# RWKV recurrence: the products of b, k with a, r over the 64 rows of their own head

## The chip, the core and the metric

The kernel runs on one core of a Trainium2 chip. The metric is the device time of one execution in microseconds (us). The core's engines run side by side and wait for each other by semaphores: TensorE (PE in the profile; PEld are its weight loads), VectorE (DVE), ScalarE (ACT), GpSimd (POOL), and SyncE (SP), which issues the DMA transfers.

## The reference, cut to what matters

A two-layer decoder trunk over 1024 tokens with 1024 features, batch 1, all in float32. Layer 0 mixes tokens with RWKV-7, layer 1 with sparse attention; each is followed by a SwiGLU. The change touches RWKV-7 alone: 16 heads of 64 features, each with a 64 x 64 state.

```python
def _rwkv7_step(S, inp):
    r_t, w_t, k_t, v_t, a_t, b_t = inp
    sa = jnp.einsum('bhij,bhj->bhi', S, a_t)
    S = S * w_t[:, :, None, :] + sa[..., None] * b_t[:, :, None, :] + v_t[..., None] * k_t[:, :, None, :]
    y = jnp.einsum('bhij,bhj->bhi', S, r_t)
    return S, y
...
    S0 = jnp.zeros((B, H, N, N), f32)
    _, y = lax.scan(_rwkv7_step, S0,
                    (tm(rh), tm(decay), tm(kh), tm(vh), tm(-kk), tm(kk * ah)))
```

## The kernel before

The tokens go in two halves of 512. Each half is first projected, with weights split into two float32r parts (L204, L121 split them; L233 to L235 are the three products), and what the recurrence needs (a, r, b, k, v, all scaled with the decay) is spilled to DRAM. Then the recurrence runs over 16 chunks of 64 tokens. It replaces the scan's steps within a chunk by products of 64 x 64 blocks and an inverse of a unit triangular block, which is computed beforehand (L630, L632, and L655 for the parts between its 32 x 32 blocks).

For a chunk, `load_chunk` brings `cbk` (b and k; feature rows of two heads in the two halves of the 128 partitions, eight pairs p of heads), `car` (a and r, 128 rows each, where for head e of a pair the other head's 64 rows are zeros, written once), `cv` (v) and `ttp` (the inverse). Then:

- `pre_chunk` makes what doesn't depend on the state. For each of the 8 pairs and both heads e, L958 multiplies `cbk[:, p]` (stationary, 128 rows x 128 columns: b's and k's 64 tokens) with `car[:, :, p, e]` (moving, a's and r's 64 tokens each). The contraction is over all 128 rows, 64 of which are the zeros. Two pairs fill one PSUM bank of tag "g". From it DVE takes the masked parts: L962 the products with a, for the 64 rows that this head uses, into `lz` (whose other 64 rows are a itself, copied by POOL at L952), and L964 those with r, into `g1`. L970 transposes `cbk` into `bk`, L978 subtracts the mean from v and puts it into `uv`.
- `chain_chunk` carries the state. L993 (z from `lz` and `uv`), a copy into zs (L995), L999 (with `ttp`), copies into `uv` (L1000, L1001), L1007 (new state from `bk` and `uv`), and L1011, L1012 (state S times its decay), copied into the next chunk's `uv` (L1015, L1016). The output is L1020 (r with the old state) plus L1023 (`g1` with `uv`), in a bank of tag "g".
- `norm` normalises the output of the chunk before: a square (L115), its sum (L1033), L1035, and yn (L1037), which reads the output's bank for the last time; L1040 transposes yn.
- After every four chunks `tail` starts: scale, bonus, gate (L1070 to L1081) and the output projection for those 256 tokens, with the residual R (L801 loads it from x, L802 scales it on DVE). It runs in steps beside the following chunks, as do the merges of the second half's inverses (L655) in the chunks 1 to 4.

PSUM has two banks each for the tags t, u, g and o in this stage. The order of the instructions on each engine is set at build time: a scheduler with a simulated timeline moves instructions where their data and a free buffer allow it. So an edit at one place can change the order at others.

Of the kernel before, what the change touches and what calls it, by code (L numbers as in the profile page):

```python
# [9 lines left out]
F32 = mybir.dt.float32  # L10
# [5 lines left out]
OP = mybir.AluOpType  # L16
# [65 lines left out]
def trunk(ctx, tc, a, out):  # L82
# [13 lines left out]
    def banks(st, name, **bufs):  # L96
        """PSUM banks of a phase by tag"""
        cur.append((pool(st, name, space=PSUM), bufs))
        st.callback(cur.pop)
# [19 lines left out]
    def sub(eng, lo, x, hi):  # L119
        """what the float32r rounding hi of x leaves"""  # L120
        i = eng.tensor_tensor(lo, x, hi.bitcast(F32), op=OP.subtract)  # L121
        (lastv if eng is V else lastg)[0] = i
# [88 lines left out]
    def wcols(w, off, ld, ncol=P):  # L211
        """weights [D, ld] as stationary tiles: columns off..off+ncol of all KT row tiles"""
        st = wst()
        dma(st[:, :KT * ncol].rearrange("p (k n) -> p k n", n=ncol), dap(w, off, [[ld, P], [P * ld, KT], [1, ncol]]))
        kp = 512 // ncol
        hi, lo = split(st, KT * ncol, kp * ncol)
        v = lambda t: [t[k // kp][:, k % kp * ncol:k % kp * ncol + ncol] for k in range(KT)]
        return v(hi), v(lo)

    def wrows(w, k0, nk, col, ld, perm=False):  # L220
        """weights as moving tiles: nk row tiles from k0, 512 columns"""
        st = wst()
        st3 = st[:, :nk * 512].rearrange("p (k n) -> p k n", n=512)
        if perm:
            for b in range(2):
                dma(st3[64 * b:64 * b + 64], dap(w, (k0 + b) * P * ld + col, [[ld, 64], [64 * ld, 2], [1, 512]]))
        else:
            dma(st3, dap(w, k0 * P * ld + col, [[ld, P], [P * ld, nk], [1, 512]]))
        hi, lo = split(st, nk * 512)
        return hi, lo  # L230
# [8 lines left out]
    def proj_fm(w, off, ld, xhi, xlo, ncol=P, c=slice(0, 512)):  # L239
        """[ncol features, tokens c]"""  # L240
        wh, wl = wcols(w, off, ld, ncol)
        o = psx(bank[0])
        for k in range(KT):
            mm3(o[:ncol, c], wh[k], wl[k], xhi[k][:, c], xlo[k][:, c], k == 0, k == KT - 1)
        return o

# [37 lines left out]
    def weave(ga, na, gb, nb):  # L284
        """two generators side by side, in proportion to their lengths"""
        ia = ib = 0
        while ga or gb:
            if ga and (not gb or ia * nb <= ib * na):
                ia += 1
                ga = None if next(ga, ga) is ga else ga  # L290
            else:
                ib += 1
                gb = None if next(gb, gb) is gb else gb

    def ada_v(l, j, stage, tmp):
        """the same with the products summed over the row tiles on VectorE"""
        acc = tmp()
        for k2 in range(4):
            st = stage()
            dma(st.rearrange("p (k n) -> p k n", n=512),  # L300
                dap(a["ada_w"], l * D * 6 * D + 2 * k2 * P * 6 * D + j * 512, [[6 * D, P], [P * 6 * D, 2], [1, 512]]))
            for i in range(2):
                k = 2 * k2 + i
                if k == 0:
                    V.tensor_scalar(acc, st[:, 0:512], csr[:, 0, 0:1], None, op0=OP.mult)
                else:
                    V.scalar_tensor_tensor(acc, st[:, i * 512:i * 512 + 512], csr[:, k, 0:1], acc, op0=OP.mult, op1=OP.add)
        mp = pst()
        for i in range(4):
            mm(mp[:, i:i + 1], acc[:, i * P:(i + 1) * P], ones, start=i == 0, stop=True, skip_group_check=True)  # L310
        V.tensor_tensor(modf[:, l, j * 4:j * 4 + 4], mp[:, 0:4], adb[l][:, j * 4:j * 4 + 4], op=OP.add)
# [11 lines left out]
    def hin_vec(l, s):  # L323
        """per feature scale and shift that take the previous LN's z (or x) to the sub-layer's input"""
# [8 lines left out]
    # position bias by head, distance descending, one row per query of a block, shifted by one place a row  # L333
# [23 lines left out]
    # the gate's second factor with its columns in the order of the normed heads  # L357
# [27 lines left out]
    def rwkv_head(hf, p1, pr, res, xq=None):  # L385
        """hin^T with the previous token in column 0, and what the low-rank branches take from it"""
# [64 lines left out]
    def rwkv_proj(hf, p1, head, between, betweenv):  # L451
# [20 lines left out]
        def low_rank_in():  # L472
            """the small operands twice: their rounding and what it leaves, over the rows of the weights' two parts"""
# [46 lines left out]
        # k  # L520
# [65 lines left out]
        # v  # L586
# [10 lines left out]
        # r  # L597
# [19 lines left out]
    def tinv_dve(hf, tp):  # L617
        """inverses of the unit triangular 64 x 64 blocks: their two 32 x 32 blocks, a unit (chunk, head) per partition"""
# [22 lines left out]
    def tinv_merge(hf, g, tp):  # L641
        """T12 = T1^T (N21^T T2^T) of 32 units, a quarter of the array for 8 of them"""
# [33 lines left out]
    with ExitStack() as st:  # L676
# [8 lines left out]
        def first_chunk():  # L685
            """the first chunk's operands, ahead of the recurrence"""
# [46 lines left out]
        # the first modulation, shift and scale of the first half of the features before those of the second  # L733
# [60 lines left out]
    def resid(l, s, hf, tt, lnt, r=None):  # L794
        """alpha * x of the sub-layer, token major"""
# [43 lines left out]
    def out_pair(w, l, s, hf, q, xh, xl, c, lnt, rr, tp, bk, perm=False, order=NK):  # L839
        """token-major product of two token tiles (columns c of x) with w [D, D], then residual and layer norm, in steps"""  # L840
# [54 lines left out]
    def hin_pair(i, q, zt, hi, lo):  # L895
        """the same for two token tiles that are still on the chip"""
# [17 lines left out]
    if True:  # L914
# [4 lines left out]
        for i in range(2):  # L919
# [3 lines left out]
            if i == 0:  # L923
                lz = [pc.tile([P, KT, 2, 64], F32, name="lz0")]
                first_g1 = [pc.tile([P, 2, P], F32, tag="g10", bufs=4, name="g1") for _ in range(4)]
# [11 lines left out]
        mask_r = cst[:, None, C_M + P:C_M + 2 * P].to_broadcast([P, 2, P])  # L937
# [10 lines left out]
        def pre_chunk(hf, c):  # L948
            """what does not depend on the state"""
# [4 lines left out]
            for p in range(0, KT, 2):  # L954
                o = psg().rearrange("p (i x e t) -> p i x e t", i=2, x=2, e=2)
                for i in range(2):
                    for e in range(2):
                        mm(o[:, i, :, e, :], cbk[:, p + i].rearrange("p a t -> p (a t)"), car[:, :, p + i, e, :], start=True, stop=True)  # L958
                g = first_g1.pop() if first_g1 else pc.tile([P, 2, P], F32, tag=f"g1{c % 2}", bufs=4, name="g1")
                for e in range(2):  # L960
                    r = slice(64 * (1 - e), 64 * (1 - e) + 64)
                    V.tensor_tensor(l_[r, p:p + 2, e, :], o[r, :, 0, e, :],  # L962
                                    cst[r, None, C_M + 64 * e:C_M + 64 * e + 64].to_broadcast([64, 2, 64]), op=OP.mult)
                V.tensor_tensor(g, o[:, :, 1].rearrange("p i e t -> p i (e t)"), mask_r, op=OP.mult)  # L964
                g1.append(g)
# [19 lines left out]
        def chain_chunk(hf, c, g1, bk, yq, state):  # L985
# [35 lines left out]
            for p in range(KT):  # L1021
                for e in range(2):
                    mm(o[64 * e:64 * e + 64, col(p)], g1[p // 2][:, p % 2, 64 * e:64 * e + 64], w_[:, e, p, :], start=False,  # L1023
# [3 lines left out]
        def norm(o, y3, yn=None):  # L1027
            """group norm, token major (the mean is already taken out of v), then feature major again, in tiles of the
            64 features of two heads of a kind, 2 * pp and 2 * pp + 2 or one more each"""
# [13 lines left out]
        def post_q(hf, q, yq, oh, ol):  # L1043
            """scale, bonus and gate for four chunks, in steps"""
            t0 = q * 256
            # the last 32 rows of either operand three times: with its rounding and what that leaves, the three parts of the product
# [38 lines left out]
        def tail(hf, q, yq):  # L1085
            """what follows the recurrence for four chunks, in steps"""
# [61 lines left out]
    def rest(gate):  # L1148
        """the tail of the last quarter, beside the next sub-layer"""
# [95 lines left out]
    with kw:  # L1245
# [15 lines left out]
        def dsa_proj(hf, tp, kih, kil, kvn, step):  # L1261
# [3 lines left out]
            # indexer keys, one copy for either head of a pair, and head weights  # L1265
# [13 lines left out]
            # indexer queries  # L1279
# [41 lines left out]
            # index scores, with the queries between them  # L1321
# [33 lines left out]
        def topk(hf):  # L1355
            """masks of the selected keys, in steps: each is sent a tile whose writing it waits for"""
# [8 lines left out]
            # the 16 high bits of the scores, as integers of the same order  # L1365
# [29 lines left out]
            # the 16 low bits, on the scores themselves: one more bit of the integer is one flipped bit of the float  # L1395
# [222 lines left out]
```

## Time and profile before

| | us |
|---|---|
| median of 3 runs (lowest, highest) | 3337.95 (3334.1, 3340.4) |
| span of the profiled execution, first to last instruction | 3331.1 |
| PE busy in the span | 3075.9 (92%) |
| DVE busy in the span | 2246.6 (67%) |
| ACT busy in the span | 1268.2 (38%) |

The profile comes from one execution of its own. Of its time it states the span alone, between the first and the last instruction; a time around that span isn't given, and the runs' median is 6.85 us above it. Lines such as L958 are those of the kernel before; the change has four lines more from L959 on, so that its L960, L964 and L967 answer to L958, L962 and L964, and from there on its lines are higher by 4.

### The profile page before, as it was taken

How to read it: one execution, taken by the hardware profiler on the slowest of the kernel's cores; microseconds unless marked ns; L12 is line 12 of the kernel's file. 1: busy time of each engine (PE TensorE's matmuls, PEld its weight loads, DVE VectorE, ACT ScalarE, POOL GpSimd, SP SyncE). 2: the span in 40 equal slices, each digit the busy share in tenths (PEclk: the TensorE clock that was granted, in tenths of full speed). 3: DMA queues.
4: the chain of work that ended last, by engine and by line, in shares of the span. 5: the costliest groups of instructions: out<-in, count | busy, mean ns of one | idle time of the engine just before them, and what ended most of it. 6: DMA issues, size and time to landing. Idle time of an engine off the chain costs nothing. (4 is left out here: it accounts for less than half of the span.)

```text
span 3331.1 us, 48910 instructions
## 1 busy us (share of the span) xinstructions
PE 3075.9 (92%) x17888; PEld 2421.7 (73%) x17888; DVE 2246.6 (67%) x4423; ACT 1268.2 (38%) x2320; POOL 989.6 (30%) x780
## 2 busy tenths in 40 slices
PE   7889698899989999999999999887999999899998
PEld 2466256688877788878888776676787777687886
DVE  4576578756766765483335787889987788775345
ACT  3552344234444222322223455552222466452223
POOL 3261135211112411241113213644222443434112
PEclk8988888999999999999999999998999999999999
DMA  6556766698864664463234432153233421253333
GB/s 194 144 168 173 129 181 169 147 175 165 193 156 126 223 194 146 126 220 95 89 103 142 132 85 68 57 161 101 90 94 108 142 66 34 89 161 102 95 98 120
DMA packets 611057, 438.42 MB, mean 132 GB/s; under 512 B 207936, under 2 KB 508480, under 8 KB 610816
## 3 DMA queue, kind: packets, MB, share of 16 engines
q1 hardware_dynamic: 610816, 435.29, 47.1%
q8 instruction: 141, 2.31, 0.3%
q14 instruction: 100, 0.82, 0.1%
HBM read 379.12 MB, written 55.95 MB: 131 GB/s over the span
## 5 line engine op out<-in xcount | busy, mean ns | idle before, releaser
L204 ACT CAST whi<-wst 128x512 fp32r<-128x512 f32 x886 | 542.1, 619 | 1374.3 <-PE psu L234 627.4
L121 POOL TENSOR_TENSOR wlo<-wst,whi 128x512 fp32r<-128x512 f32 x330 | 457.3, 1386 | 1531.9 <-ACT whi L204 1505.5
L121 DVE TENSOR_TENSOR wlo<-wst,whi 128x512 fp32r<-128x512 f32 (+1 forms) x556 | 476.7, 862 | 476.7 <-ACT whi L204 467.8
L233 PE MATMUL psu<-hin,whi 128*128 128x512 f32 (+1 forms) x1568 | 588.5, 376 | 52.3 <-DVE sl L1171 47.2
L234 PE MATMUL psu<-hin,whi 128*128 128x512 f32 (+1 forms) x1568 | 586.3, 374 | 8.1 <-DVE hin L907 4.7
L235 PE MATMUL psu<-hin,wlo 128*128 128x512 f32 (+1 forms) x1568 | 584.5, 373 | 0.0
L233 PEld LDWEIGHTS psu<-hin,whi 128*128 128x128 f32 x1568 | 302.6, 193 | 107.8 <-DVE sl L1171 52.0
L234 PEld LDWEIGHTS psu<-hin,whi 128*128 128x128 f32 x1568 | 303.0, 193 | 59.4 <-DVE hin L907 5.2
L235 PEld LDWEIGHTS psu<-hin,wlo 128*128 128x128 f32 x1568 | 302.9, 193 | 49.6
L233 PE MATMUL psg<-whi,hid 128*128 128x512 f32 x528 | 206.4, 393 | 3.4 <-DVE fl L1393 3.4
L234 PE MATMUL psg<-wlo,hid 128*128 128x512 f32 x528 | 207.1, 392 | 0.0
L235 PE MATMUL psg<-whi,hid 128*128 128x512 f32 x528 | 206.5, 392 | 0.0
L233 PE MATMUL psg<-xs,whi 128*128 128x512 f32 x384 | 163.3, 434 | 18.9 <-ACT whi L204 10.7
L234 PE MATMUL psg<-xs,whi 128*128 128x512 f32 x384 | 163.2, 426 | 9.1 <-DVE xs L121 4.6
L235 PE MATMUL psg<-xs,wlo 128*128 128x512 f32 x384 | 161.0, 421 | 1.2 <-DVE wlo L121 1.2
L1171 DVE TENSOR_TENSOR sl<-sl,psu 128x512 f32<-128x512 f32 (+1 forms) x98 | 61.7, 630 | 140.8 <-PE psu L235 130.6
L233 PEld LDWEIGHTS psg<-whi,hid 128*128 128x128 f32 x528 | 99.6, 189 | 25.0 <-issue 3.8
L233 PEld LDWEIGHTS psg<-xs,whi 128*128 128x128 f32 x384 | 77.5, 203 | 52.1 <-ACT whi L204 14.4
L234 PEld LDWEIGHTS psg<-wlo,hid 128*128 128x128 f32 x528 | 99.6, 189 | 21.7 <-DVE R L813 0.4
L235 PEld LDWEIGHTS psg<-whi,hid 128*128 128x128 f32 x528 | 99.5, 188 | 21.4
L115 ACT ACTIVATE z<-z,mx 128x128 f32<-128x128 f32 (+7 forms) x128 | 99.2, 776 | 33.1 <-DVE mx L1521 32.2
L234 PEld LDWEIGHTS psg<-xs,whi 128*128 128x128 f32 x384 | 77.0, 200 | 39.1 <-issue 10.6
(416 smaller groups left out, 6484.8 us busy)
## 6 DMA issues: line engine op xcount, KB each, us to landing
wst<-in_ffn_w_in_dram SPq DMA_DIRECT2D x196, 512.0 KB
wst<-in_ffn_w_out_dram SPq DMA_DIRECT2D x92, 512.0 KB
wst<-in_rwkv_w_rkv_dram SPq DMA_DIRECT2D x48, 512.0 KB
z<-in_ada_w_dram SPq DMA_DIRECT2D x48, 512.0 KB
wst<-in_ada_w_dram SPq DMA_DIRECT2D x32, 512.0 KB
wst<-in_rwkv_w_out_dram SPq DMA_DIRECT2D x64, 256.0 KB
wst<-in_dsa_w_out_dram SPq DMA_DIRECT2D x32, 512.0 KB
wst<-in_dsa_w_in_dram SPq DMA_DIRECT2D x26, 512.0 KB
```

The lines of the kernel that those rows point to most:

```text
L115: return A.activation(o, i, f, **kw)
L121: i = eng.tensor_tensor(lo, x, hi.bitcast(F32), op=OP.subtract)
L204: A.copy(h_[:, :m], st[:, c:c + m])
L233: mm(o, lh, rh, start=first, stop=False)
L234: mm(o, lh, rl, start=False, stop=False)
L235: mm(o, ll, rh, start=False, stop=last)
L1171: V.tensor_tensor(sl[:, c], sl[:, c], ou[:, c], op=OP.mult)
```

## The change

The contraction runs over the 64 rows of a head's own half. `cbk[r, p]` and `car[r, :, p, e]` are taken with r the rows 0 to 63 for e = 0 and 64 to 127 for e = 1, so that two products lie in two row halves of the array. Each half writes a bank of its own: four pairs of one head fill a bank, and two banks are asked for together. The masks follow: per chunk four of 64 x 256 into `lz` and four of 128 x 256 into `g1`, in place of eight of 64 x 128 and four of 128 x 256. `g1` is kept per head, and L1023 (L1027 in the change) reads it accordingly. The zero rows of `car` stay, as L1020 still uses them. Comments and docstrings left out by the change are not shown.

```diff
-                first_g1 = [pc.tile([P, 2, P], F32, tag="g10", bufs=4, name="g1") for _ in range(4)]
+                first_g1 = [pc.tile([P, 4, 64], F32, tag="g10", bufs=4, name="g1") for _ in range(4)]
...
-        mask_r = cst[:, None, C_M + P:C_M + 2 * P].to_broadcast([P, 2, P])
+        mask_r = cst[:, None, C_M + P:C_M + P + 64].to_broadcast([P, 4, 64])
...
             g1 = []
-            for p in range(0, KT, 2):
-                o = psg().rearrange("p (i x e t) -> p i x e t", i=2, x=2, e=2)
-                for i in range(2):
+            for p in range(0, KT, 4):
+                o = [psg().rearrange("p (i x t) -> p i x t", i=4, x=2) for _ in range(2)]
+                for i in range(4):
                     for e in range(2):
-                        mm(o[:, i, :, e, :], cbk[:, p + i].rearrange("p a t -> p (a t)"), car[:, :, p + i, e, :], start=True, stop=True)
-                g = first_g1.pop() if first_g1 else pc.tile([P, 2, P], F32, tag=f"g1{c % 2}", bufs=4, name="g1")
+                        r = slice(64 * e, 64 * e + 64)
+                        mm(o[e][:, i], cbk[r, p + i].rearrange("p a t -> p (a t)"), car[r, :, p + i, e, :], start=True, stop=True)
+                gs = []
                 for e in range(2):
                     r = slice(64 * (1 - e), 64 * (1 - e) + 64)
-                    V.tensor_tensor(l_[r, p:p + 2, e, :], o[r, :, 0, e, :],
-                                    cst[r, None, C_M + 64 * e:C_M + 64 * e + 64].to_broadcast([64, 2, 64]), op=OP.mult)
-                V.tensor_tensor(g, o[:, :, 1].rearrange("p i e t -> p i (e t)"), mask_r, op=OP.mult)
-                g1.append(g)
+                    V.tensor_tensor(l_[r, p:p + 4, e, :], o[e][r, :, 0, :],
+                                    cst[r, None, C_M + 64 * e:C_M + 64 * e + 64].to_broadcast([64, 4, 64]), op=OP.mult)
+                    g = first_g1.pop() if first_g1 else pc.tile([P, 4, 64], F32, tag=f"g1{c % 2}", bufs=4, name="g1")
+                    V.tensor_tensor(g, o[e][:, :, 1, :], mask_r, op=OP.mult)
+                    gs.append(g)
+                g1.append(gs)
...
-                    mm(o[64 * e:64 * e + 64, col(p)], g1[p // 2][:, p % 2, 64 * e:64 * e + 64], w_[:, e, p, :], start=False,
+                    mm(o[64 * e:64 * e + 64, col(p)], g1[p // 4][e][:, p % 4, :], w_[:, e, p, :], start=False,
                        stop=p == KT - 1, **sk)
```

The order of the built program on PE, where the recurrence begins: the first chunk's products (ctbk_4767, ctar_4768), before. A row is the line, the operation, what it writes and reads (psg, pst, psu are PSUM tiles by tag, each with its number), its size and how often it follows itself.

```order
L958 MATMUL psg_5230<-ctar0_4768,ctbk0_4767 128x2x64 x4
L958 MATMUL psg_5238<-ctar0_4768,ctbk0_4767 128x2x64 x4
L970 MATMUL pst_5262<-cst_61,ctbk0_4767 128x128 x4
L970 MATMUL pst_5268<-cst_61,ctbk0_4767 128x128 x4
L978 MATMUL pst_5274<-cst_61,ctv0_5197 64x64 x16
L958 MATMUL psg_5246<-ctar0_4768,ctbk0_4767 128x2x64 x4
L958 MATMUL psg_5254<-ctar0_4768,ctbk0_4767 128x2x64 x4
L993 MATMUL psu_5293<-uv0_5195,lz0_5198 64x64
```

The same place in the change, from the last of four pairs of the first eight products on; the tile with the even number belongs to the first head's rows, the odd one to the second's at first, and psg_5244 and psg_5245 are the next two.

```order
L960 MATMUL psg_5230<-ctar0_4768,ctbk0_4767 128x128
L960 MATMUL psg_5231<-ctar0_4768,ctbk0_4767 128x128
L974 MATMUL pst_5258<-cst_61,ctbk0_4767 128x128 x4
L974 MATMUL pst_5264<-cst_61,ctbk0_4767 128x128 x4
L982 MATMUL pst_5270<-cst_61,ctv0_5197 64x64 x16
L960 MATMUL psg_5244<-ctar0_4768,ctbk0_4767 128x128 x4
L960 MATMUL psg_5245<-ctar0_4768,ctbk0_4767 128x128 x4
L997 MATMUL psu_5289<-uv0_5195,lz0_5198 64x64
```

The first eight products change between the two tiles one by one; the second eight come as four of one tile and four of the other.

PE a little later, the second chunk's products (ctbk1_5210) among the first chunk's chain, before:

```order
L993 MATMUL psu_5293<-uv0_5195,lz0_5198 64x64 x15
L958 MATMUL psg_5390<-ctar1_5211,ctbk1_5210 128x2x64
L978 MATMUL pst_5440<-cst_61,ctv1_5207 64x64 x16
L999 MATMUL psu_5312<-zs_5310,ttp0_5196 64x64 x16
L958 MATMUL psg_5390<-ctar1_5211,ctbk1_5210 128x2x64 x3
L1007 MATMUL psu_5331<-uv0_5195,bk_5204 64x64
L1023 MATMUL psg_5355<-uv0_5195,g1_5202 64x64
L1007 MATMUL psu_5331<-uv0_5195,bk_5204 64x64 x7
```

And in the change:

```order
L997 MATMUL psu_5289<-uv0_5195,lz0_5198 64x64 x15
L960 MATMUL psg_5386<-ctar1_5211,ctbk1_5210 128x128 x4
L982 MATMUL pst_5432<-cst_61,ctv1_5207 64x64 x12
L1003 MATMUL psu_5308<-zs_5306,ttp0_5196 64x64 x16
L960 MATMUL psg_5387<-ctar1_5211,ctbk1_5210 128x128 x4
L982 MATMUL pst_5432<-cst_61,ctv1_5207 64x64 x4
L1011 MATMUL psu_5327<-uv0_5195,bk_5204 64x64
L1027 MATMUL psg_5351<-uv0_5195,g1_5202 64x64
```

The four products of the first head's rows (psg_5386) and the four of the second's (psg_5387) stand apart, with other products between them; all later chunks look like this.

DVE at the end of the third group of four chunks, where the residual R is scaled (L802) while the last chunk's output waits for its norm, before:

```order
L964 TENSOR_TENSOR g_8555<-psg,cst 128x256
L1035 RECIPROCAL rv<-rv 128x8
L802 TENSOR_SCALAR R<-R 128x1024
L1037 TENSOR_TENSOR yn<-psg,rv 128x512
L962 TENSOR_TENSOR lz_5198<-psg,cst 64x2x64 x2
L964 TENSOR_TENSOR g_8564<-psg,cst 128x256
L995 COPY zs<-psu 128x512
```

And in the change:

```order
L967 TENSOR_TENSOR g_8511<-psg,cst 128x256
L1039 RECIPROCAL rv<-rv 128x8
L1041 TENSOR_TENSOR yn<-psg,rv 128x512
L964 TENSOR_TENSOR lz_5198<-psg,cst 64x4x64
L967 TENSOR_TENSOR g_8514<-psg,cst 128x256
L802 TENSOR_SCALAR R<-R 128x1024
L999 COPY zs<-psu 128x512
```

yn and the next masks have moved ahead of L802; the copy into zs is still behind it.

## Rows read from the trace of the kernel before

**Rows 1.** The page's head: span, busy us by engine, granted clock by slice.
```profile
span 3331.1 us, 48910 instructions
...
PE 3075.9 (92%) x17888; PEld 2421.7 (73%) x17888; DVE 2246.6 (67%) x4423; ACT 1268.2 (38%) x2320; POOL 989.6 (30%) x780
...
PEclk8988888999999999999999999998999999999999
```

**Rows 2.** Busy time in stretches: the recurrence's first four chunks, the rest, all.
```profile
core 0: us, PE busy (x) PEld busy (x) DVE busy (x) ACT busy (x) POOL busy (x), PEclk, DMA share, GB/s
659.00:745.00 86.00, 77.06 (x1342) 69.62 (x1342) 48.77 (x118) 32.02 (x64) 8.04 (x14) 0.92 1.00 181
745.00:1009.00 264.00, 241.57 (x3296) 211.02 (x3294) 180.04 (x398) 114.57 (x214) 44.31 (x56) 0.94 0.81 170
659.00:1009.00 350.00, 318.63 (x4636) 280.64 (x4636) 228.81 (x516) 146.59 (x278) 52.36 (x69) 0.94 0.85 173
```

**Rows 3.** PE's waits from 659 to 1009 us: total us, times, longest.
```profile
PE psg L1020 <- DVE yn L1037: 10.5, 2, 5.7
...
PE psu L993 <- DVE lz L962: 1.4, 3, 0.7
...
PE psg L1020 <- DVE g L964: 1.1, 1, 1.1
PE psg L958 <- DVE g L964: 0.9, 3, 0.3
```

**Rows 4.** The edited lines: count, shortest/median/longest ns, first and last start, forms.
```profile
L958 PE MATMUL psg<-ctar,ctbk x512: 269/275/582, 659.4 to 998.6; 128*128 128x128 f32 x171
...
L962 DVE TENSOR_TENSOR lz<-psg,cst x128: 282/289/297, 664.6 to 1001.6; 64x128 f32<-64x128 f32 x128
...
L964 DVE TENSOR_TENSOR g<-psg,cst x64: 405/406/411, 665.4 to 1001.9; 128x256 f32<-128x256 f32 x64
...
L999 PE MATMUL psu<-zs,ttp x512: 222/222/270, 673.9 to 1004.6; 128*64 128x64 f32 x171
```

**Rows 5.** PE's timeline at full clock: start us, us, line, size, records in a row.
```profile
685.27 0.75 PE L1020 MATMUL psg<-S,ctar 128*64 128x64 f32 x20
685.96 0.49 PE L958 MATMUL psg<-ctar,ctbk 128*128 128x128 f32 x2
686.28 0.60 PE L970 MATMUL pst<-cst,ctbk 128*128 128x128 f32 x4
686.81 0.68 PE L978 MATMUL pst<-cst,ctv 128*64 128x64 f32 x14
687.42 0.71 PE L958 MATMUL psg<-ctar,ctbk 128*128 128x128 f32 x4
688.06 1.15 PE L999 MATMUL psu<-zs,ttp 128*64 128x64 f32 x32
```

**Rows 6.** PE's timeline earlier: one tile of 64 x 64, and L568's form.
```profile
546.55 1.87 PE L568 MATMUL pst<-sp 64*64 64x64 f32 x32 [1.33 <-DVE sp L556]
...
L568 PE MATMUL pst<-sp x512: 218/218/365, 164.8 to 548.2; 64*64 64x64 f32 x171
```

**Rows 7.** PE and DVE at the second and third quarter's end: idle before, releaser.
```profile
842.07 0.69 DVE L802 TENSOR_SCALAR R<-R 128x1024 f32<-128x1024 f32 x1 [5.37 <-DMA R<-in_x_dram]
...
843.66 1.55 PE L1020 MATMUL psg<-S,ctar 128*64 128x64 f32 x24 [4.84 <-DVE yn L1037]
...
927.79 0.69 DVE L802 TENSOR_SCALAR R<-R 128x1024 f32<-128x1024 f32 x1 [5.80 <-DMA R<-in_x_dram]
928.40 0.68 DVE L1037 TENSOR_TENSOR yn<-psg,rv 128x512 f32<-128x512 f32 x1
...
929.14 1.76 PE L1020 MATMUL psg<-S,ctar 128*64 128x64 f32 x28 [5.69 <-DVE yn L1037]
```

**Rows 8.** Stretches as in rows 2; the last row is L655 alone.
```profile
690.80:697.60 6.80, 6.80 (x162) 6.31 (x159) 4.32 (x10) 4.13 (x10) 0.98 (x2) 1.00 1.29 204
...
700.00:710.00 10.00, 10.00 (x134) 9.24 (x135) 3.66 (x10) 3.65 (x9) 0.00 (x0) 0.61 0.97 237
926.00:934.00 8.00, 4.86 (x56) 4.75 (x56) 3.60 (x8) 0.58 (x1) 0.00 (x0) 0.57 1.05 330
...
690.80:697.60 6.80, 2.64 (x70) 2.20 (x66) 1.00 1.29 204
```

## Prediction, made before the change was run

> **What bounds the kernel now.** I read the page's head first: TensorE (PE) is busy 92% of a span of 3331.1 us, VectorE (DVE) 67% [rows 1]. The edit touches only the RWKV recurrence, so next comes the busy time by stretch. The recurrence runs from about 659 to 1009 us, 350 us for 16 chunks, 21.9 us each. PE is busy 318.63 us of it, DVE 228.81 us (65%), and the granted clock averages 0.94 [rows 2]. So PE is the bound here, with 31 us of idle time. The list of PE's waits says what the idle time is: 10.5 us in two waits of L1020 for DVE's yn (L1037), and little pieces; the rows that name the edited operations (L958 for g, L993 for lz, L1020 for g) come to 0.9 + 1.4 + 1.1 = 3.4 us [rows 3]. What counts is therefore PE's own time in the recurrence, and how long PE stands at the two long waits.
>
> **What the edited products cost now.** L958 is 16 products a chunk, 256 in all, and each is two records: 512 [rows 4]. Their recorded duration of 275 ns is pipeline length. The cost is the distance between starts: four records in a row last 0.71 us, so after a first distance of 0.215 (explained below) two distances take 0.71 - 0.275 - 0.215 = 0.22 us, 0.11 each [rows 5]. 512 x 0.11 = 56 us of PE, 3.5 us a chunk. Two row halves side by side could at best save half, 28 us.
>
> **Do the halves run side by side?** The diff alternates the halves, product by product, between two banks. The built order doesn't, as the sections of order above show: only the first eight products of the first chunk alternate. From then on the scheduler issues four products of one half, other work, and then four of the other half. The reason is in the kernel: tag "g" has two banks, and the chunk's output (psg of L1020/L1023) keeps one until yn (L1037) has read it. The two tiles that the new pre_chunk asks for take the other bank in turn. I counted the whole order: 8 products alternate, 248 stand in runs of one half. Gain of the alternation: 8 x 2 records x 0.11 / 2 = 0.9 us.
>
> **What four products of one half cost.** A 64 x 128 fp32 run in one half isn't in the trace. Nearest row: L568 works on 64 x 64 of the array, 32 records in 1.87 us with a last one of 0.218, so (1.87 - 0.218) / 31 = 0.0533 us for 64 moving columns [rows 6]. For 128 columns that is 0.107, against 0.11 now: the zero rows cost no time, and leaving them out alone saves nothing (bounds: 0 and 0.003 x 512 = 1.5 us; I take 0).
>
> **What the new array shape costs.** Neighbouring products differ in how much of the array they use, and a change shows in the starts [rows 5]. L970 (128 x 128), four records in 0.60 us and so (0.60 - 0.275) / 3 = 0.108 apart, starts at 686.28; L978 (128 x 64) should start at 686.71 and starts at 686.81: +0.10. L999's 32 records, too, take 1.15 us where L1020's pace of (0.75 - 0.222) / 19 = 0.028 gives 1.09: +0.06. Into 128 x 128, L1020's 20 records end at 685.27 + 20 x 0.028 = 685.83, and L958 starts at 685.96: +0.13, of which I count 0.10 as in the other direction; its second record comes 0.49 - 0.275 = 0.215 after its first instead of 0.11: +0.10. So a change into full width costs 0.20 us, one into half width 0.16. The same shape costs nothing: L958 at 685.96, two records, 0.215 + 0.11, and L970 is there at 686.28. Before, L958 shares its shape with the transposes and the background products; afterwards its 64 x 128 shape is that of nothing else. Counted in both orders, from the first L958 to the recurrence's end: 201 changes before, 238 after. Of those after, 51 lie between 64 x 128 and 128 x 128, where there was no change. The others fall: into half width 91 to 84, into full width from half width 76 to 75, the others, with 32 x 32 products, by 6 (0.1 each, the drain alone). Sum: 51 x 0.2 - 7 x 0.16 - 0.2 - 0.6 = +8.3 us. Whether 64 x 128 to 128 x 128 costs as much as the 128 x 64 to 128 x 128 of the rows is open: bounds 0 (then the sum is -1.9) and 0.2; I take 0.2, the nearest row. With the alternation: +7.4 us, and as 9% of PE's time is idle, +6.7.
>
> **VectorE.** Per chunk, eight masks of 64 x 128 (289 ns) and four of 128 x 256 (406 ns) [rows 4], 3.94 us, become four of 64 x 256 and four of 128 x 256. 64 x 256 isn't in the trace: 0.406 (as many elements per partition; nearest) to 0.578 (two of the old). With 0.406 it is 3.25 us: 0.69 less a chunk, 11 us in all. DVE is not the bound; only the 3.4 us of [rows 3] can come back. I take 1 (bounds 0 and 3.4). In the runs of four, a half's products also wait for its own half of ctar only, while before one product went ahead and three waited; that is inside those waits.
>
> **The moved wait.** The scheduler has set DVE's order anew, and one place matters. At the second and third quarter's end DVE stands on L802, which waits for the residual R: 5.37 and 5.80 us. yn stands behind it, and PE stands for 4.84 and 5.69 us on the bank that yn frees [rows 7]. At the third the new order has yn ahead of L802, by the order section; at the second L802 stays in front. DVE still waits for R, but PE then has L1020 (16 products, 0.9), the rest of L993 (0.2), yn's transposes (0.44), the next L958 (0.9) and four L970 (0.44): 2.9 us, after which it needs zs, which DVE copies behind L802. So -2.9 us (bounds 0 and -5.7). The half clock there (0.57 granted between 926 and 934 [rows 8]) may go with it, another 3.
>
> **Sum.** +6.7 - 1 - 2.9 = +2.8 us. The profile shows a span of 3331.1 us; the median of the runs is 3337.95, 6.9 above it, which I take as what lies around the span. 3337.95 + 2.8 = 3340.7. 0.2% is 6.7 us, about what a measurement of this kernel tells from no change: I forecast no change that it can tell.
>
> **Rivals.**
> 1. *Slower, because PE's clock falls more often.* Between 690.8 and 697.6 us PE was busy throughout, 2.64 us of it with 32 x 32 products (L655); the granted clock then went from 1.00 to 0.61 in the ten us from 700 [rows 8]. Work on a small part of the array, then, did not hold the clock as full work does. 64 x 128 takes 3.5 us a chunk from full to half. With full-price changes (+7.4) and one more fall like that one (half clock for some 8 us, 4 us lost), and the long waits unmoved: 3337.95 + 11.4, about 3350. It decides from one further fall on. Against it: the rest of the chunk stays as it is. 0.29.
> 2. *Weight loads of one half don't hide.* Each record would then come as late as the second after a change: +0.10 on 7 of 8 records of 63 runs, 441 x 0.10 = 44 us on top of the forecast: 3385. L568's 0.0533 [rows 6] speaks against it, loads of one tile behind each other at the pace of the columns. 0.03. The Trainium skill, "TensorE: Matmul & The Clock Gate", Part 3 (What overlaps and what doesn't), says that a weight load overlaps running products only where the row group differs; by that rule this rival would hold. The L568 row disagrees.
> 3. *Faster, by the moved wait.* All 5.7 us of the third wait go, its half clock too (3), and changes between full-width shapes cost little (about -1): 3328. For it: [rows 7]; against: the zs copy is still behind L802. 0.16.
> 4. *The halves overlap after all,* in spite of the order. The price is shown by column halves: L999's 32 records of 64 columns in 1.15 us, (1.15 - 0.222) / 31 = 0.030, against 0.0533 for one tile [rows 5, 6]. A record would fall to 0.11 x 0.030 / 0.0533 = 0.062 and save 512 x 0.048 = 25 us, less the 0.9 counted: 3317. Against: runs of four of one half, in one bank, with a DVE round between. 0.05. The Trainium skill, "TensorEngine Tiling (Array Packing)", Tiling Modes (Key Properties), says that different tiles load and multiply in parallel; by it the diff as written would give these 25 us, the built order only the 0.9.
>
> **Numbers.** My forecast has 0.47 (own range 3331.5 to 3344.5); slower 0.29 + 0.03; faster 0.16 + 0.05. The range 3328 to 3351 takes in rivals 1 and 3 and leaves out 2, 4 and their like.
>
> **What would show it.** In the changed kernel: L960's records 0.107 to 0.11 apart inside a run, 512 of them and some 56 us; 0.2 us lost at each entry from 128 x 128 work; DVE 11 us less busy in the recurrence; PE's wait for yn at the third quarter's end gone or below 3 us, that at the second still some 5. I am wrong if records inside a run are 0.06 or 0.2 apart, if changes between the two full-width shapes cost nothing, or if the granted clock between 659 and 1009 moves by more than 0.02.

## The result, and the profile after

The change is slower: 3355.76 us median of 5 runs (3351.42 to 3368.48) against 3337.95 of 5 runs before (3328.56 to 3340.40), a ratio of 1.006 with a 95% interval of 1.004 to 1.008: some 18 us more. That lies above the forecast (3340.7) and above its range (to 3351).

The page's head of the changed kernel, as in [rows 1]:

```profile
span 3349.6 us, 48847 instructions
...
PE 3091.0 (92%) x17888; PEld 2429.8 (73%) x17888; DVE 2239.0 (67%) x4359; ACT 1269.3 (38%) x2320; POOL 990.1 (30%) x780
...
PEclk8989898987999999999999998998999999999999
```

TensorE does as many matrix products as before and is busy 15 us longer; VectorE has 64 instructions and 8 us less. The clock line has a new dip: in the ninth and tenth slice (84 us each, 670 to 837 us), where the recurrence begins, 9 and 9 became 8 and 7. The stretches of [rows 2], and two more that divide it at 790 us:

```profile
core 0: us, PE busy (x) PEld busy (x) DVE busy (x) ACT busy (x) POOL busy (x), PEclk, DMA share, GB/s
659.00:745.00 86.00, 74.84 (x1241) 67.66 (x1240) 44.80 (x94) 30.80 (x61) 7.79 (x13) 0.84 0.93 175
745.00:1009.00 264.00, 249.12 (x3222) 212.63 (x3221) 165.25 (x331) 108.36 (x205) 41.27 (x52) 0.89 0.77 162
659.00:1009.00 350.00, 323.97 (x4461) 280.29 (x4460) 210.04 (x425) 139.16 (x265) 49.06 (x65) 0.87 0.81 165
...
659.00:790.00 131.00, 117.47 (x1848) 105.53 (x1847) 63.93 (x137) 45.87 (x95) 13.02 (x21) 0.79 0.90 164
790.00:1009.00 219.00, 206.50 (x2617) 174.75 (x2615) 146.12 (x288) 93.28 (x171) 36.03 (x44) 0.93 0.75 166
```

The granted clock of the whole stretch fell from 0.94 to 0.87. The records show two levels, 1.2 GHz (0.50) and 2.4 GHz (1.00), so a mean of 0.87 over 350 us means 2 x 0.13 x 350 = 91 us at the half clock, against 2 x 0.06 x 350 = 42 before. At the half clock eight records of L960 take 2.07 us (at 786.57) instead of 1.16 (at 863.54, below), so about half of the difference, 24 us, is lost: the 350 us end 175 of TensorE's records earlier in the program (4636 before, 4461 now), and from the first of the edited products to the last it takes 356.8 us (658.3 to 1015.1, below) where it took 339.2 [rows 4], 17.6 more. Nearly all of it is lost before 790 us, where the merges of the second half's inverses (L655) run beside the chunks 1 to 4: 0.91 before, 0.79 now. The same two stretches before:

```profile
659.00:790.00 131.00, 118.98 (x1999) 107.40 (x2000) 75.70 (x181) 51.41 (x109) 13.21 (x22) 0.91 0.95 169
790.00:1009.00 219.00, 199.65 (x2639) 173.23 (x2637) 153.11 (x335) 95.18 (x170) 39.15 (x47) 0.95 0.79 175
```

Two short stretches of the change at the half clock:

```profile
core 0: us, PE busy (x) PEld busy (x) DVE busy (x) ACT busy (x) POOL busy (x), PEclk, DMA share, GB/s
...
757.00:775.00 18.00, 16.72 (x226) 15.29 (x226) 7.39 (x18) 5.70 (x13) 1.54 (x3) 0.53 0.71 121
781.00:802.00 21.00, 21.00 (x185) 17.74 (x184) 9.54 (x21) 6.23 (x16) 1.21 (x2) 0.51 0.66 134
```

In the last row TensorE waited for nothing in 21 us, and yet ran at the half clock. The waits do not add up to the loss: of the 350 us TensorE is idle 26, and was 31 before. The longest of them (total us, times, longest; from 659 to 1030 us, as the recurrence now ends later):

```profile
PE pso L1078 <- DVE whi L121: 7.7, 1, 7.7
PE psg L1024 <- DVE yn L1041: 4.6, 1, 4.6
PE psu L997 <- ACT rv L115: 3.4, 1, 3.4
PE psu L1003 <- DVE zs L999: 2.5, 2, 1.5
```

The two waits for yn (10.5 us, [rows 3]) have become one, and a wait of 7.7 us at the gate's product (L1078) is new. It ends at 713.73 us, and the trace's clock stands at half from 709.5 to 726.6, so this fall goes with an idle TensorE:

```profile
713.73 0.80 PE L1078 MATMUL pso<-sgh,whi 96*128 96x256 f32 x2 [7.66 <-DVE whi L121]
```

In the two stretches above it was idle for 1.28 us and not at all. The edited lines, as in [rows 4]:

```profile
L960 PE MATMUL psg<-ctar,ctbk x512: 272/272/580, 658.3 to 1015.1; 64*128 64x128 f32 x171
...
L964 DVE TENSOR_TENSOR lz<-psg,cst x64: 403/422/428, 663.5 to 1016.1; 64x256 f32<-64x256 f32 x64
...
L967 DVE TENSOR_TENSOR g<-psg,cst x64: 402/414/426, 664.2 to 1016.4; 128x256 f32<-128x256 f32 x64
```

TensorE's timeline at full clock, beside [rows 5] (start us, us, line, size, records in a row):

```profile
862.83 0.78 PE L1044 MATMUL pst<-cst,yn 128*128 128x128 f32 x4
863.54 1.16 PE L960 MATMUL psg<-ctar,ctbk 64*128 64x128 f32 x8
864.63 0.66 PE L974 MATMUL pst<-cst,ctbk 128*128 128x128 f32 x4
```

From L960's first start to L974's is 1.09 us for 8 records. At 0.11 each they would take 0.88; the other 0.21 are L960's second record, which comes 0.1 late after the change of shape, and the next shape's start, another 0.1 late. At the two ends the same shows: L960 starts 0.20 after the last of L1044's four (863.34), 0.09 more than 0.11, and L974's four take 0.66 in place of 0.60. In and out together cost 0.09 + 0.21 + 0.06 = 0.36 us, 0.18 a change.

### The profile page after: what moved, and what is told of

The parts are those of the page before. It is cut to its first block, busy times and chain, and to the rows that moved or that the text cites. A ratio compares the mean times of both kernels' runs of the same rounds, so it can differ in the third digit from the quotient of the medians.

```text
span 3349.6 us, 48847 instructions
## 1 busy us (share of the span) xinstructions
PE 3091.0 (92%) x17888; PEld 2429.8 (73%) x17888; DVE 2239.0 (67%) x4359; ACT 1269.3 (38%) x2320; POOL 990.1 (30%) x780
## 5 line engine op out<-in xcount | busy, mean ns | idle before, releaser
L121 POOL TENSOR_TENSOR wlo<-wst,whi 128x512 fp32r<-128x512 f32 x330 | 454.9, 1379 | 1555.6 <-ACT whi L204 1515.0
L121 DVE TENSOR_TENSOR wlo<-wst,whi 128x512 fp32r<-128x512 f32 (+1 forms) x556 | 472.8, 855 | 487.9 <-ACT whi L204 479.0
L233 PE MATMUL psg<-xs,whi 128*128 128x512 f32 x384 | 164.0, 436 | 18.4 <-ACT whi L204 10.7
```

What stands on the lines that cost most here:

```text
L233: mm(o, lh, rh, start=first, stop=False)
```

## Experiments

Each was run in five rounds beside the kernel before, which gave 3338.1, 3338.8 and 3338.1 us in the three sets (32, 26 and 23 runs). Every run also states its mean granted clock over the whole execution. (1 - clock) x time is the time lost to the half clock, at most, since it counts idle stretches too; what is left is work and waits. Medians of time, means of clock (the means are good to 0.0003 to 0.0013, that is 1 to 4 us; before has 0.9555 and 0.9554 in the other two sets). A profile is one execution, and that can lie some 10 us off its kernel's median (e8 3342.9 us, e7 3342.6, e5 3325.2, e1 3345.2), so the table decides how much, and the profiles tell where:

| kernel | us (runs) | ratio to before, 95% | clock | lost to it, us | rest, us |
|---|---|---|---|---|---|
| before | 3338.1 (32) | | 0.9557 | 147.9 | 3190.2 |
| the change | 3355.8 (5) | 1.004 to 1.008 | 0.9486 | 172.5 | 3183.3 |
| e1_full_rows | 3339.2 (12) | 0.9994 to 1.0018 | 0.9546 | 151.6 | 3187.6 |
| e7_rows_late | 3349.1 (12) | 1.0022 to 1.0054 | 0.9529 | 157.7 | 3191.4 |
| e8_rows_early | 3355.8 (5) | 1.0033 to 1.0066 | 0.9496 | 169.1 | 3186.7 |
| e4_before_spread | 3327.2 (9) | 0.9956 to 0.9985 | 0.9579 | 140.1 | 3187.1 |
| e3_after_spread | 3337.4 (12) | 0.9988 to 1.0016 | 0.9554 | 148.8 | 3188.6 |
| e9_full_with_changes | 3342.6 (12) | 0.9996 to 1.0019 | 0.9550 | 150.4 | 3192.2 |
| e11_full_twice | 3380.2 (5) | 1.0099 to 1.0135 | 0.9562 | 148.1 | 3232.1 |
| e10_rows_twice | 3384.9 (6) | 1.0126 to 1.0182 | 0.9535 | 157.4 | 3227.5 |
| e5_col_halves | 3340.8 (12) | 0.9984 to 1.0011 | 0.9542 | 153.0 | 3187.8 |
| e6_col_halves_spread | 3327.8 (9) | 0.9951 to 0.9977 | 0.9586 | 137.8 | 3190.0 |
| e2_two_tags | 3344.5 (12) | 1.0009 to 1.0037 | 0.9498 | 167.9 | 3176.6 |
| e2b_two_tags_spread | 3331.7 (12) | 0.996 to 0.9983 | 0.9551 | 149.6 | 3182.1 |

The change's 18 us are thus +24.6 lost to the clock and -6.9 of the rest. The theories: the 64-row products lose the clock (rows); the shape changes do (changes); or the new order and its waits cost the time (order).

**Full rows in the change's layout** (e1):

```diff
-                        mm(o[e][:, i], cbk[r, p + i]..., car[r, :, p + i, e, :], start=True, stop=True)
+                        mm(o[e][:, i], cbk[:, p + i]..., car[:, :, p + i, e, :], start=True, stop=True)
```

> The change with only its row halves undone: the same banks, masks and fours, but each product contracts over all 128 rows (zeros included) again. Theory A (the clock: 64-row products let PE's clock fall for longer; in the profile of the change 88.7 us of the recurrence stand at half clock against 44.9 before, some 20 us lost): about 45 us at half clock again and 3334 to 3342 us. Theory B (the new order and its waits cost the time, whatever the rows): 3350 to 3360 us, with half clock near 85 us. Theory C (changes of the array's shape cost it): also back to about 3340, but then full-clock work plus gaps in the recurrence would be less than the 299.9 us of the change, by 8 us or more, with the half clock hardly moved.

Back at the time and the clock of before, with the banks, the masks and `g1` per head still there, so those don't cost the 17 us. The order is not quite the same, though: the scheduler has built another one. By the two traces, some 200 of TensorE's 4492 instructions from the first of these products to the last stand elsewhere, all of them between 725 and 837 us of the change, among the merges, where the clock was lost. So e1 by itself does not part the rows from the order. Two runs below help: in e7 TensorE has e1's order, in e8 that of the change, but for at most 3 instructions.

**Changes of shape without 64-row work** (e9, on e1):

```diff
+                        if e == 0 and i == 2:
+                            mm(o[e][:, i, 0, 0:4], cbk[r, p + i]..., car[r, 0, p + i, e, 0:4], start=True, stop=True)
```

> The change's layout with full-row products (3339.2 us when run alone), plus one extra product over 64 rows with 4 moving columns in the middle of every run of the first head (32 in all; its output is overwritten). It adds 62 shape changes to the order (193 to 255; the change itself has 238) and next to no 64-row work. Theory 'rows left out lose clock': the clock stays that of full rows (0.955 over the whole execution, half clock some 49 us) and the time grows by the changes alone, 62 x 0.1 to 0.2, 6 to 12 us: 3345 to 3351. Theory 'the shape changes themselves, the little drains, lose the clock': mean clock falls to 0.949 as with the change, half clock 75 to 90 us, and the time is 3356 to 3366.

Its timeline (L961 is the extra product, L962 the full ones):

```profile
685.79 0.61 PE L962 MATMUL psg<-ctar,ctbk 128*128 128x128 f32 x4
686.33 0.38 PE L961 MATMUL psg<-ctar,ctbk 64*128 64x4 f32 x2
686.64 0.71 PE L962 MATMUL psg<-ctar,ctbk 128*128 128x128 f32 x4
```

The second four would start at 685.79 + 4 x 0.11 = 686.23; they start 0.41 later, and take 0.71 instead of 0.61: 0.51 us each time, 32 x 0.51 = 16 us of TensorE. Yet the clock is that of full rows, and the time 3.4 us above e1, less than expected; by the ratios (1.0007 and 1.0006) it can't be told from e1's. So the changes alone do not lose the clock. That most of what they cost TensorE went into time that it would have waited is likely, but not shown.

**Where in the recurrence** (e7: 64 rows from the seventh chunk on; e8: in the first six chunks only):

```diff
-                        r = slice(64 * e, 64 * e + 64)
+                        r = slice(64 * e, 64 * e + 64) if hf * 8 + c > 5 else slice(0, 128)
```

> The change's layout, but the products of b, k with a, r contract over 64 rows only from the seventh chunk on (10 of 16 chunks); in the first six they take all 128 rows, zeros too. The 64 rows everywhere gave 3355.8 us, the full rows everywhere 3339.2, a difference of 16.6. Theory 'the 64-row products hold the clock badly only beside the 32 x 32 merges' (chunks 1 to 4, where the change lost most): 3339 to 3342 us, half clock in the recurrence some 50 us, as with full rows. Theory 'they cost clock wherever they are': 10/16 of 16.6, about 3349, half clock some 74 us. Theory 'shape changes': +2.5 us, about 3342, with the half clock unmoved.

> The counterpart: 64 rows in the first six chunks only, full rows in the other ten. Theory 'only beside the 32 x 32 merges': 3352 to 3356 us, half clock some 85 us, nearly all of it before 790 us. Theory 'wherever they are': 6/16 of 16.6, about 3345, half clock some 64 us. Theory 'shape changes': +1.5 us, about 3341, half clock unmoved.

e8 has the whole loss (3355.8), as the nearness to the merges wants. As its order is that of the change, it shows that full rows in the last ten chunks give back nothing that can be told there. Its clock by stretch:

```profile
659.00:790.00 131.00, 114.59 (x1762) 101.80 (x1760) 65.19 (x141) 43.99 (x90) 13.84 (x23) 0.80 0.89 158
790.00:1009.00 219.00, 204.99 (x2754) 179.05 (x2754) 154.12 (x308) 99.05 (x181) 39.90 (x47) 0.97 0.78 172
```

That of e7:

```profile
659.00:790.00 131.00, 114.79 (x1940) 103.49 (x1941) 72.11 (x153) 49.83 (x105) 13.09 (x21) 0.91 0.91 167
790.00:1009.00 219.00, 206.71 (x2667) 174.33 (x2665) 152.91 (x300) 94.53 (x170) 40.59 (x48) 0.95 0.79 171
```

With full rows beside the merges, and e1's order, the first stretch is back at 0.91. But e7 is no 3340, it is 3349.1, 9.9 us above e1, with 6 more lost to the clock, and the intervals of the two ratios don't meet. The order is the same, so here the 64 rows, with the changes of shape that they bring, cost by themselves. Where they cost it the profile of e7 doesn't show, as that execution was one of the quick ones; its runs spread most (3339 to 3371). Neither expectation holds for both kernels. Over e1 the two lose 9.9 + 16.6 = 26.5 us against the change's 16.6, but by the clock 6.1 + 17.5 = 23.6 against 20.9: with errors of several us, the losses can't be told from a plain sum.

For the early chunks no pair of runs has the same order and other rows: the change's order with full rows there was not run. What there is are several orders. The stretch from 659 to 790 us in e1, e9, e2 and e10 (the last two come below), in this turn:

```profile
659.00:790.00 131.00, 108.66 (x1824) 97.10 (x1822) 68.69 (x145) 45.26 (x94) 14.47 (x24) 0.87 0.91 162
659.00:790.00 131.00, 117.54 (x1951) 104.96 (x1952) 69.86 (x150) 50.15 (x105) 12.16 (x20) 0.93 0.91 164
659.00:790.00 131.00, 112.11 (x1788) 100.43 (x1788) 64.72 (x137) 46.72 (x98) 11.99 (x19) 0.78 0.86 159
659.00:790.00 131.00, 117.70 (x1832) 106.42 (x1832) 59.69 (x128) 41.41 (x84) 13.07 (x23) 0.90 0.81 150
```

With full rows beside the merges the clock is 0.87 to 0.93 in the three orders of before, e1 and e7, and e9. With 64 rows it is 0.78 to 0.80 in two, that of the change and e8 and that of e2, but 0.90 in the order of e10. So the rows are the likely cause of the early loss, and the order decides how much of it comes.

**The merges moved**, spread out over the chunks 4, 6, 8 and 10 (e4 in the kernel before, e3 in the change):

```diff
-            if 1 <= gc < 5:
-                tinv_merge(1, gc - 1, pc)
+            if gc in (4, 6, 8, 10):
+                tinv_merge(1, gc // 2 - 2, pc)
```

> The kernel before with the same move of the merges. Control for the run above: theory A (merges among full-row products were the cause of the first three falls, 23.8 us at half clock): 20 to 35 us at half clock, 3328 to 3336 us. Theory B: no different from before, 3335 to 3342 us, or slower by new waits.

> The change with the four merges of 32 x 32 products moved from chunks 1 to 4 to chunks 4, 6, 8 and 10, where the tail's full-array products run beside them. Theory A, if the fall needs 32 x 32 and 64-row products close together: half clock in the recurrence falls from 88.7 to 60 us or less, 3338 to 3348 us. If the 64-row products alone bring it: half clock stays at 80 or more, 3350 to 3360 us.

The move alone gives the kernel before 10.9 us, a version faster than both kernels. The change gains more by it, 18.4 us, with 23.7 less lost to the clock, so the merges in the chunks 1 to 4 take part in its loss. Between the two with the merges spread out, the change costs 10.2 us (8.7 of clock): less than 17.7, not nothing. The 64-row products are still in the chunks that now have the merges; whether it is the wider spacing that helps or the tail's full-array products beside them, these two runs don't tell.

**Twice as much of the same product** (e10 on the change, e11 on e1):

```diff
+                        for _ in range(2):
-                        mm(o[e][:, i], ...
+                            mm(o[e][:, i], ...
```

> The change with each of the 64-row products issued twice to the same output (512 more records, 0.107 apart: 55 us more PE work, of which 91% shows: 50). Read against the same doubling with full rows. Theory 'rows left out lose clock, in proportion to the 64-row work': the gap to the full rows doubles from 16.6 to some 33 us: 3390 + 33, about 3423, half clock 130 us. Theory 'shape changes' (248 against 188 in the order): the gap stays about 17 or grows to 20: 3407 to 3410.

> The change's layout with full rows and each product issued twice: 3339.2 + 50, about 3389 to 3391 us, half clock near 49 us or below by either theory, since more of the time is full-array work.

Here the theory of the rows missed in size. The two have the same order on TensorE but for some dozen of 18400 instructions, so the rows alone differ. The gap is 4.7 us by the medians, 9.3 by the clock, and by the ratios (1.0154 and 1.0117) 12, give or take 11. A gap of 33 is excluded, one of 17 is not: the loss is not in proportion to the 64-row work, and whether it is smaller than the change's stays open. Both kernels kept a higher clock than the change (in the first stretch 0.90 each); their order, or more work between the merges, may be why, but no run tells.

**Half the columns in place of half the rows** (e5 on the kernel before; e6 with the merges moved as well):

```diff
-                        mm(o[:, i, :, e, :], cbk[:, p + i]..., car[:, :, p + i, e, :], start=True, stop=True)
+                        for h in range(2):
+                            mm(o[64 * h:64 * h + 64, i, :, e, :], cbk[:, p + i, h, :], car[:, :, p + i, e, :], start=True, stop=True)
```

> The kernel before with each of these products cut into two column halves (64 columns of b, 64 of k; all 128 rows, two output halves in one bank), next to each other in the order, so the products have the shape of most of their neighbours. Twice as many records (1024), at the pace of the 128 x 64 rows of before (0.028 us for 64 moving columns, so 0.056 for 128): 57 us against 56, no gain from that. Theory 'what a product covers of the array decides on the clock, and half of it, rows or columns, holds it less': half clock up as with the change, 3345 to 3356 us. Theory 'only rows left out lose clock': half clock near 45 us as before, and fewer shape changes (201 to 183 in the order, 0.2 each) give 3 us: about 3335. If the column halves don't run side by side: +56 us, 3394.

> The same column halves with the merges of the second half's inverses in the chunks 4, 6, 8 and 10 instead of 1 to 4; the kernel before with that move alone gave 3327.2 us with 21 us of half clock. Theory 'only rows left out lose clock': 3 us less from fewer shape changes, about 3324, half clock some 21 us. Theory 'any half of the array': half clock up by some 30 us as with row halves and the same move, about 3337 to 3340.

No loss of clock that can be told (0.9542 against 0.9557, and 0.9586 against 0.9579), and no gain in time from fewer shape changes either. A product that fills half the array by columns, with its other half right behind it, behaves like a full one. It is no pure comparison of columns with rows: the column halves run side by side (else the time had been near 3394), the row halves of the change mostly don't.

**The halves really side by side** (e2: the second head's bank from another tag; e2b: and the merges moved):

```diff
-                o = [psg().rearrange("p (i x t) -> p i x t", i=4, x=2) for _ in range(2)]
+                o = [f().rearrange("p (i x t) -> p i x t", i=4, x=2) for f in (psg, pst)]
```

> The change with its second row half in a bank of tag t instead of g, so that the two halves can be asked for side by side: in the built order 121 neighbours alternate between the halves instead of 8. If halves side by side run at the same time, alternating records stand about 0.06 us apart on average instead of 0.11 and PE works up to 20 us less. Theory A (clock): side by side the whole array is in use again, so half clock falls to 45 to 65 us and the time to 3320 to 3340 us. Theory B (order and waits): bank t is now shared with transposes and merges, so new waits, 3345 to 3360 us.

> The change with the two row halves in banks of two tags (so that 105 products alternate and run side by side; with the merges in the chunks 1 to 4 that was 3344.5 us, 15 us less full-clock work and 30 us more half clock) and the merges in the chunks 4, 6, 8 and 10. Theory 'rows left out lose clock, worst beside the 32 x 32 merges': the clock comes back to that of the change with the merges moved (0.955), the saved work stays: 3344.5 - 18, about 3326, near the best kernel so far (3327). Theory 'two tags cost waits (38.7 us idle) whatever the merges do': 3333 to 3338.

e2's timeline, where the two halves' products now alternate:

```profile
686.58 0.27 PE L960 MATMUL psg<-ctar,ctbk 64*128 64x128 f32 x1
686.58 0.27 PE L960 MATMUL pst<-ctar,ctbk 64*128 64x128 f32 x1
686.69 0.27 PE L960 MATMUL psg<-ctar,ctbk 64*128 64x128 f32 x1
686.69 0.27 PE L960 MATMUL pst<-ctar,ctbk 64*128 64x128 f32 x1
```

Two records start together every 0.11 us. So the two halves do run at the same time, 0.055 us a record. The Trainium skill, "TensorEngine Tiling (Array Packing)", Tiling Modes (Key Properties), says that different tiles load and multiply in parallel; these rows agree. The rest falls by 13.6 us to 3176.6, but 20 us more go to the clock, so theory A fails: half of the records side by side (132 pairs of the 512 start together) did not bring the clock back. Two waits are new:

```profile
PE pst L1044 <- DVE yn L1041: 15.5, 3, 6.9
PE pst L655 <- ACT bk L976: 8.2, 1, 8.2
```

With the merges moved (e2b) the clock comes back, and the kernel beats before by 6.4 us. Its time lies between the two expectations, as the rest is 3182.1, 5.5 above that of e2. By the ratios (0.9972 and 0.9970) it can't be told from e4, the same move without the 64 rows.

## Why the prediction was wrong

**The step that failed is the clock.** The sum took the granted clock as that of the kernel before. Rival 1 named a mechanism, work on a small part of the array that doesn't hold the clock, and gave it 0.29, but priced it at one more fall, 8 us of half clock, 4 us lost. The runs show 24.6 us more lost, six times that. "The rest of the chunk stays as it is", the argument against it, was no protection: with full rows the clock held in every order that was run (0.9546 to 0.9579 over the execution), and the order of the rest did not stay. The prediction's own test, a granted clock between 659 and 1009 us that moves by more than 0.02, gave 0.07.

How far the cause is shown: that the 64 rows cost at all, by e7 against e1, which differ in the order by 3 instructions at most (9.9 us; their kernels before agree to 0.7); that the merges take part, by e3 and e2b, where the change and e2 get 24 and 18 us of clock back by moving them. That the rows are what loses the clock among the early merges fits all runs, but there the order differs with the rows, and in the order of e10 little was lost. The share of each stays open.

**What lies around the span:** the sum took 6.9 us, the median less the profiled span. In the runs of the change and the experiments that were profiled, the time is 1.8 us above the span (3351.42 and 3349.6). By that the other 5 are one quick execution against the median. The forecast starts from the median, so it didn't suffer.

**Records of one half:** right. Eight records of L960 take 1.16 us at full clock, and those inside a run 0.11 each, not 0.06 and not 0.2; the zeros cost no time, and rival 2 fell. The Trainium skill, "TensorE: Matmul & The Clock Gate", Part 3 (What overlaps and what doesn't), wants another row group for a weight load to overlap; these rows disagree, as those of L568 did: one row half, and still the pace of full rows.

**Side by side:** right that the built order undoes it, and rival 4's price (0.062) was near what e2 then showed (0.055).

**Shape changes, +8.3 us:** the price of 0.2 for a change between 64 x 128 and 128 x 128 was right where it can be read (0.18, from 862.83 on), and the order has the changes that were counted. The way to the total was not shown to be right. The prediction let 91% of it show. In e9 3.4 of 16 us did, and the change's rest lies below that of e1 by 4.3, within the error of the two.

**VectorE, -11 us:** the masks took 16 x (8 x 0.289 + 4 x 0.406) = 63.0 us and take 16 x (4 x 0.422 + 4 x 0.414) = 53.5, so -9.5; off the path, as said. What it is worth was not measured by itself.

**The moved wait, -2.9 us** (bounds 0 and -5.7): DVE and TensorE at the two places of [rows 7]:

```profile
858.48 0.69 DVE L802 TENSOR_SCALAR R<-R 128x1024 f32<-128x1024 f32 x1 [4.88 <-DMA R<-in_x_dram]
...
860.07 1.98 PE L1024 MATMUL psg<-S,ctar 128*64 128x64 f32 x32 [4.58 <-DVE yn L1041]
...
941.36 0.69 DVE L1041 TENSOR_TENSOR yn<-psg,rv 128x512 f32<-128x512 f32 x1
...
947.76 0.69 DVE L802 TENSOR_SCALAR R<-R 128x1024 f32<-128x1024 f32 x1 [4.99 <-DMA R<-in_x_dram]
...
949.11 1.15 PE L1003 MATMUL psu<-zs,ttp 128*64 128x64 f32 x32 [1.45 <-DVE zs L999]
```

At the third quarter's end yn goes first, and the next wait is for zs, as described: 5.69 us became 1.45, -4.2. At the second it stays (4.84, now 4.58). What I did not see is the new wait before 713.73 us, where TensorE stands 7.7 us at L1078 on DVE's whi (L121); it takes back what the yn waits gave. e1 has it too (7.4) and is no slower than before.

**Open:** how much of the early loss belongs to the rows and how much to the order around the merges (the change's order with full rows would tell), why the loss doesn't grow with the 64-row work (e10), and why 64 rows in the late chunks cost 9.9 us in e1's order and nothing that can be told in the change's (e8).

## What to carry to other kernels

Rows of zeros in a contraction are not waste to be removed for its own sake: here they cost no time per product, and with the same products over half the rows the recurrence stood at the half clock for twice as long (91 us and 42). Before giving products half the array's rows, look for work on small tiles beside them and read the granted clock there. The cheaper step was to spread the small-tile work out (e4, 0.997), which no wait in the profile asked for. And when a control run undoes one part of a change, compare its built order with the change's before calling that part the cause.

## What the hardware showed unexpectedly

- A TensorE that is busy throughout does not have the full clock for that: 21.00 of 21.00 us busy at 0.51, with 64-row, 32 x 32 and full products in turn.
- Rows that hold zeros count: with them in the last ten chunks the time is 3339.2 us, without them 3349.1 (e1 and e7, the same order).
- Half the columns, side by side, did not lose what half the rows lost, mostly one after the other (a clock of 0.9542 and 0.9486).
- Two 64-row products in the two halves start within 0.01 us of each other and 0.11 us before the next two, in banks of different tags (e2).
